# Feed-forward of a hybrid trunk layer on one core: eight block products or seven, all tokens at once or two sets of them

## The chip, the core and the metric

The kernel runs on one core of a Trainium2 chip. The engines are named as the profile names them: PE (matrix products, with PEld for its weight loads), DVE (vector engine), ACT (scalar engine), POOL (GpSimd) and SP (here only a queue of DMAs). The metric is the device time of one execution in microseconds, the median of several runs.

## The reference

One layer of a streaming trunk for 1040 prompt tokens (16 learned meta tokens and 1024 new ones) and 32 sample tokens, model width 1024, feed-forward width 2816. A token mixer (attention, pooling, a scan) comes first and is the same in both kernels. What the change touches is the second half of the layer:

```python
x = x + rmsnorm(mix @ w_out, ln_post_mix)
h = rmsnorm(x, ln_pre_ffn)
ff = (jax.nn.silu(h @ w_gate) * (h @ w_up)) @ w_down
x = x + rmsnorm(ff, ln_post_ffn)
```

All inputs are fp32. The feed-forward's result is needed for 1056 tokens (32 sample, 1024 prompt): the rows of the meta tokens are dropped.

## The kernel before

**Arithmetic.** Every fp32 operand of a product is split in two fp32r numbers, `hi` (a rounded copy, made on ACT by `hi_of`, line 47) and `lo` (the rest, made on DVE by `lo_of`, line 53, or on POOL by `lo_of_sbuf`, line 56). A product of two operands is three matmuls, hi·hi, hi·lo and lo·hi (`PASSES`, line 37), summed in PSUM.

**Stages.** Phase A is the in-projection, the scan and the pooling, phase B the attention, phase C the out-projection with both norms (lines 1215 to 1487), phase D the feed-forward (from line 1304). Phase C works on nine token tiles: 48 rows, then eight of 128. For each it takes the out-projection's products (`c_products`), adds, norms and scales on DVE, ACT and POOL, and turns the result with PE transposes (`c_turn`, line 1292) into `T`, features by tokens, split into hi and lo. `T` is first the out-projection's operand and then, tile by tile, the feed-forward's.

**Feed-forward.** The 2816 features are 22 tiles of 128, the tokens three chunks of 288, 384 and 384 (`FCH`). For a feature tile `f`, `gu_weights` (line 1385) loads gate and up weights, 512 KB each, and splits them: two copies of 128x1024 on ACT, two subtractions of 128x1024 on DVE. `gu_products` (line 1394) takes 24 matmuls for each chunk and each of gate and up; `gu_act` (line 1405) does silu on ACT, the product with up on DVE, and splits the result into `act`. For two feature tiles `down_weights` (line 1498) splits the down weights and `down` (line 1507) takes, for each chunk and each of the 8 tiles of outputs, six matmuls, whose result DVE adds to `acc` in SBUF (line 1520). The last two feature tiles go chunk by chunk, so that the ends of the token tiles (`final_tile`, `last_tile`) run beside products.

**Order.** Each engine executes its instructions in the order of its own list. PE's list in phases B and C is set by hand by the order of the code; the loops over the feed-forward are laid down in the order of the code, and a scheduler orders the other engines' lists. PSUM has eight banks: four for products of gate and up and for turns, four for the down products.

## Time and profile before

| | |
|---|---|
| median of 3 runs | 1409.21 us (1408.17 to 1415.13) |
| profiled execution | span 1416.8 us from its first to its last instruction; the page shows no other time for it |
| PE busy | 1322.6 us, 93% of the span |
| DVE, ACT, POOL busy | 639.2, 398.5, 205.1 us |
| feed-forward's matmuls in the profile | gate and up 3168, down 1536 and 36 at the end |
| first of them | at 626.59 us after the span's start |

Lines of a group of instructions read: source line, engine, operation, out<-in by the program's names, shape of the output and of the input, count, then busy time in us, mean ns of one, and the idle time of the engine just ahead of them with what ended it. Lines of the timeline read: start in us, duration in us (of the whole piece where several instructions are merged), engine, line, operation, and in brackets the idle time ahead of it. A table of windows gives for each stretch the busy us of every engine.

### The profile page before, as it was taken

Reading aid. Unit: us, or ns where it says so; the run is one execution under the profiler, and the core shown is the slowest. Engines: PE = TensorE matmul, PEld = TensorE weight load, DVE = VectorE, ACT = ScalarE, POOL = GpSimd, SP = SyncE. Lnnn points to the kernel's source line nnn. Section 1 sums busy time; section 2 is a strip of 40 time slices with the busy share of each in tenths; the row PEclk is TensorE's granted clock in tenths of the full one; section 3 lists DMA queues with packets and bytes.
Section 4 is the critical chain, followed back from the end, with each engine's and each line's share of the span. In section 5 each row is a group of like instructions: output and inputs, shape, how many; then the busy total and the mean of one; then the engine's idle time right before and its main releaser. Section 6 shows DMA issues by size and latency. Waiting matters only on the chain. (4 is left out here: it accounts for less than half of the span.)

```text
span 1416.8 us, 19972 instructions
## 1 busy us (share of the span) xinstructions
PE 1322.6 (93%) x7898; PEld 1236.0 (87%) x7898; DVE 639.2 (45%) x1209; ACT 398.5 (28%) x868; POOL 205.1 (14%) x311
## 2 busy tenths in 40 slices
PE   7999999999695596999999999999999999999996
PEld 6999788878574473779999999999999999999996
DVE  4578774554552141675525251515152424243356
ACT  7332442443543252443111111111111120212013
POOL 1001672101031221672000000000000000000024
PEclk9999999999897797999999999999999999999999
DMA  8320457989989835645111110111110111110024
GB/s 296 118 83 24 134 165 243 175 137 140 161 136 164 157 69 157 219 171 165 46 44 57 34 60 31 60 31 60 31 60 31 60 30 60 31 59 19 16 79 149
DMA packets 87089, 140.30 MB, mean 99 GB/s; under 512 B 19670, under 2 KB 63724, under 8 KB 86996
## 3 DMA queue, kind: packets, MB, share of 16 engines
q1 hardware_dynamic: 86996, 139.03, 38.7%
q8 instruction: 62, 1.02, 0.3%
q14 instruction: 31, 0.25, 0.1%
HBM read 103.66 MB, written 35.34 MB: 98 GB/s over the span
## 5 line engine op out<-in xcount | busy, mean ns | idle before, releaser
L60 PE MATMUL gu<-T,wgu 128*128 128x384 f32 (+1 forms) x3168 | 514.3, 323 | 1.9 <-ACT fs L1411 1.3
L60 PEld LDWEIGHTS gu<-T,wgu 128*128 128x128 f32 x3168 | 509.7, 188 | 2.5 <-ACT fs L1411 1.6
L60 PE MATMUL dn<-act,HD 128*128 128x384 f32 (+1 forms) x1536 | 248.1, 322 | 0.0
L60 PEld LDWEIGHTS dn<-act,HD 128*128 128x128 f32 x1536 | 246.4, 188 | 0.0
L60 PE MATMUL wk<-T,wkh 128*128 128x384 f32 (+1 forms) x1152 | 208.5, 334 | 1.3 <-POOL wkh L57 0.8
L60 PEld LDWEIGHTS wk<-T,wkh 128*128 128x128 f32 x1152 | 190.2, 192 | 4.4 <-POOL wkh L57 1.1
L1412 DVE TENSOR_TENSOR fs<-fs,gu 128x384 f32<-128x384 f32 (+1 forms) x66 | 34.3, 520 | 332.8 <-PE gu L60 332.6
L1520 DVE TENSOR_TENSOR acc<-acc,dn 128x384 f32<-128x384 f32 (+1 forms) x232 | 117.9, 518 | 86.3 <-PE dn L60 85.1
L69 POOL TENSOR_SCALAR est<-est 128x1 f32<-128x1 f32 (+1 forms) x9 | 3.6, 397 | 726.6 <-ACT ey L1324 723.0
L60 PE MATMUL o<-PT,H 128*128 128x256 f32 (+1 forms) x324 | 64.6, 316 | 26.7 <-ACT ot L1097 15.9
L54 DVE TENSOR_TENSOR PT<-t,PT 128x512 fp32r<-128x512 f32 (+2 forms) x96 | 50.4, 530 | 64.6 <-ACT PT L49 63.3
L49 ACT ACTIVATE HD<-dr 128x1024 fp32r<-128x1024 f32 x22 | 22.3, 1054 | 203.3 <-PE dn L60 200.2
L60 PEld LDWEIGHTS o<-PT,H 128*128 128x128 f32 x324 | 50.2, 208 | 33.6 <-ACT ot L1097 17.1
L49 ACT ACTIVATE act<-fs 128x384 fp32r<-128x384 f32 (+1 forms) x66 | 32.5, 493 | 160.3 <-DVE fs L1412 160.2
L1411 ACT ACTIVATE fs<-gu 128x384 f32<-128x384 f32 (+1 forms) x66 | 30.7, 465 | 162.8 <-PE gu L60 162.8
L49 ACT ACTIVATE wgu<-gr 128x1024 fp32r<-128x1024 f32 (+1 forms) x48 | 47.1, 982 | 72.7 <-PE gu L60 72.7
L60 PE MATMUL s<-H 64*128 64x512 f32 (+5 forms) x180 | 65.8, 378 | 0.9 <-DMA H<-qd 0.9
L49 ACT ACTIVATE PT<-t 128x512 fp32r<-128x512 f32 (+2 forms) x96 | 44.1, 468 | 79.7 <-PE t L1063 49.8
L60 PE MATMUL wp<-wo,T 128*128 128x512 f32 (+1 forms) x162 | 51.4, 443 | 14.3 <-ACT pp L931 14.3
L1018 DVE CUSTOM_DVE_ANT_0 S<-s,H,pinf 128x512 f32<-128x512 f32 (+4 forms) x54 | 34.6, 640 | 64.6 <-PE s L60 59.3
L1063 PE MATMUL t<-ident,S 128*128 128x128 f32 x264 | 48.0, 292 | 14.3 <-DVE st L1018 8.8
L1063 PEld LDWEIGHTS t<-ident,S 128*128 128x128 f32 x264 | 30.1, 143 | 26.7 <-issue 16.2
(231 smaller groups left out, 1347.2 us busy)
## 6 DMA issues: line engine op xcount, KB each, us to landing
gr<-in_wgu_dram SPq DMA_DIRECT2D x40, 512.0 KB, 4.7
dr<-in_wd_dram SPq DMA_DIRECT2D x22, 512.0 KB, 3.6
wkr<-in_wx_dram SPq DMA_DIRECT2D x16, 512.0 KB, 6.3
H<-qd SPq DMA_DIRECT2D x18, 268.0 KB, 7.2
xt<-in_x_dram SPq DMA_DIRECT2D x8, 512.0 KB, 7.0
wor<-in_w_out_dram SPq DMA_DIRECT2D x8, 512.0 KB, 7.3
ppd<-pp SPq DMA_DIRECT2D x8, 512.0 KB, 10.5
cp<-ppd SPq DMA_DIRECT2D x8, 512.0 KB, 3.9
```

What stands on the lines that cost most here:

```text
L49: nc.scalar.activation(out, in_, AF.Copy)
L54: nc.vector.tensor_tensor(out=out, in0=in_, in1=hi.bitcast(F32), op=ALU.subtract)
L60: return nc.tensor.matmul(out, lhsT, rhs, start=start, stop=stop, skip_group_check=True)
L69: gp.tensor_scalar(v, ssq, ssq2, n * EPS, op0=ALU.add, op1=ALU.add)
L1018: nc.vector.tensor_tensor_reduce(out=Sf[:R, PAD + j0:PAD + j0 + n], in0=ps[:R, :n], in1=bc[:R, k0 + j0:k0 + j0 + n].bitcast(F32), scale=1. ...
L1063: nc.tensor.transpose(ps[:, c:c + P], tiles[h, t][0][:, P * b:P * b + P], ident)
L1411: nc.scalar.activation(s[:, :n], pg[:, :n], AF.Silu)
L1412: nc.vector.tensor_mul(s[:, :n], s[:, :n], pu[:, :n])
L1520: nc.vector.tensor_add(dst, dst, ps[:, :n])
```

## The change

The feed-forward's three products are taken by a scheme of seven block products (the Strassen-Winograd form). Each matrix is cut in 2x2 blocks; sums and differences of blocks of each operand are formed, seven products are taken instead of eight, and sums of the products give the four result blocks.

- **Tokens** come in two sets, one after the other: set 0 has 544 tokens as two blocks of 272 (the sample tokens and prompt tiles 1 to 4), set 1 has 512 as two of 256 (tiles 5 to 8). Both sets go through all weights, so that all weights are loaded, summed and split twice.
- **Units.** A gate-up unit takes two feature tiles: 7 block products of 24 matmuls each (two halves f by four k by three passes), each [128x128] by [128x272] or [128x256]. A down unit takes four feature tiles (two in the first group of set 0 and in the last of set 1): 7 block products of 24 matmuls (12 in the two short ones). A set has 11 gate-up units and 6 down units, in the order gate-up, gate-up, down after the start.
- **Weights** (`w_steps`): per unit four loads of 512 KB, four sums of blocks on POOL (128x1024 each), seven splits, each a copy of 128x1024 on ACT and a subtraction of 128x1024 on DVE. They are made in seven steps, the first five beside the unit before.
- **Tokens' operand** (`h_steps`): four sums of blocks (DVE and POOL), seven splits of 128x1088 or 128x1024, once for each set. It lies in `T`, over the out-projection's operand. Set 1's blocks wait in DRAM (`h1d`).
- **Evictions.** In a gate-up unit, products 1 and 2 add up in one PSUM tile, 6, 7 and 4 in a second, 5 and 3 in a third; DVE or ACT reads each stage of the running sum before the next product goes on top of it. The results' four blocks give four more differences on POOL (128x272 or 128x256) and seven split blocks `AO`. In a down unit DVE adds 14 pieces of 128x544 or 128x512 from PSUM to `acc`, 7 blocks by 4 tiles.
- **Ends.** After the last down unit of a set seven sums of blocks of `acc` are made on DVE, and the token tiles end as before (`final_piece`): set 0's beside the first units of set 1, set 1's at the end of the program.
- Four small tiles of one column to nine become slices of one. Up to the middle of the out-projection every engine's list is otherwise the same in both kernels.

The core of the diff, with comment lines left out:

```diff
+FSET = (272, 256)
+ORDER7 = (1, 2, 6, 7, 4, 5, 3)
...
+    def h_steps(s, blocks, spare):
+        H = h_ops(s)
+        b11, b12, b21, b22 = blocks
+        dv, gp, sb = nc.vector, nc.gpsimd, ALU.subtract
+        def split(i, raw):
+            split_raw(H[:, i - 1, 0], H[:, i - 1, 1], raw)
+        split(1, b11)
+        dv.tensor_tensor(out=b11, in0=b12, in1=b11, op=sb)
+        yield
+        split(2, b21)
+        dv.tensor_tensor(out=spare, in0=b22, in1=b11, op=sb)
+        gp.tensor_tensor(out=b21, in0=b21, in1=spare, op=sb)
+        yield
+        split(6, spare)
+        gp.tensor_tensor(out=b12, in0=b22, in1=b12, op=sb)
...
+    def w_steps(unit, nm, W):
...
+        split_raw(*ring(1), a11)
+        gp.tensor_tensor(out=a11, in0=a11, in1=a21, op=ALU.subtract)
+        yield
+        split_raw(*ring(2), a12)
+        yield
+        s2 = S6[:, :na]
+        gp.tensor_tensor(out=s2, in0=a22, in1=a11, op=ALU.subtract)
+        gp.tensor_tensor(out=a12, in0=a12, in1=s2, op=ALU.subtract)
+        split_raw(*ring(6), s2)
+        gp.tensor_tensor(out=a21, in0=a21, in1=a22, op=ALU.add)
+        yield
+        split_raw(*ring(7), a11)
+        yield
+        for i in ORDER7[4:6]:
+            split_raw(*ring(i), a21 if i == 5 else a22)
+            yield
+        split_raw(*ring(3), a12)
+        yield
...
-    def gu_products(f, ci, g):
-        c0, n = FCH[ci]
-        ps = psum("mm", f"gu{f}_{g}_{c0}")
-        for k in range(NK):
-            for j, (i0, i1) in enumerate(PASSES):
-                mm(ps[:, :n], gus[f][:, i0, 8 * g + k], T[:, i1, k, c0:c0 + n],
-                   k == 0 and j == 0, k == NK - 1 and j == 2)
-        return ps
+    def gu_unit(s, W, p, par, between):
...
+        def prod(ps, i, start, after):
+            for f in range(2):
+                for k in range(4):
+                    for j, (i0, i1) in enumerate(PASSES):
+                        mm(ps[:, f, :n], W[i][:, i0, f, k * P:(k + 1) * P], H[:, i - 1, i1, k * n:(k + 1) * n],
+                           start and k == 0 and j == 0, k == 3 and j == 2)
+                after(ps[:, f, :n], f)
+            between()
+        def plus(out, other):
+            return lambda ps, f: dv.tensor_tensor(out=out[:, f], in0=ps, in1=other[:, f], op=add)
+        X = pair_psum("gx")
+        prod(X, 1, True, lambda ps, f: nc.scalar.activation(m1[:, f], ps, AF.Copy))
+        prod(X, 2, False, lambda ps, f: nc.scalar.activation(g0[:, f], ps, AF.Silu))
+        Y = pair_psum("gy")
+        prod(Y, 6, True, plus(u2, m1))
+        prod(Y, 7, False, plus(u3, m1))
+        prod(Y, 4, False, plus(m1, m1))
...
+        dv.tensor_tensor(out=m1, in0=g0, in1=m1, op=ALU.mult)
+        split(2, 4, m1)
+        Z = pair_psum("gz")
+        prod(Z, 5, True, plus(u3, u3))
+        def c12(ps, f):
+            plus(u2, u2)(ps, f)
+            nc.scalar.activation(u2[:, f], u2[:, f], AF.Silu)
+            dv.tensor_tensor(out=u2[:, f], in0=u2[:, f], in1=u3[:, f], op=ALU.mult)
+        prod(Z, 3, False, c12)
...
+        gp.tensor_tensor(out=t1, in0=b12, in1=b11, op=sb)
+        gp.tensor_tensor(out=t2, in0=b22, in1=t1, op=sb)
+        gp.tensor_tensor(out=t3, in0=b22, in1=b12, op=sb)
+        gp.tensor_tensor(out=t4, in0=b21, in1=t2, op=sb)
+        split(6, 8, g0)
+        split(4, 6, u3)
+        split(1, 2, u2[:, 1:2])
+    def down_unit(s, W, np_, first, between, after=None):
+        n = FSET[s]
+        for i in ORDER7:
+            for jj in range(2):
+                ps = pair_psum("dn")
...
+                dst = acc[:, i - 1, 2 * jj:2 * jj + 2, :n]
+                if first:
+                    nc.scalar.activation(dst, ps[:, :, :n], AF.Copy)
+                else:
+                    nc.vector.tensor_tensor(out=dst, in0=ps[:, :, :n], in1=dst, op=ALU.add)
...
+    def combine(s):
+        for o, x in ((2, 1), (6, 1), (3, 6), (7, 6), (4, 7), (3, 5), (5, 7)):
+            acc_add(s, o, x)
+            yield
...
+        def between():
+            n_between[0] += 1
+            step(preps[si])
+            if hgen is not None:
+                step(hgen)
+            if si == 0 and n_between[0] <= 3:
+                c_stage(8 + n_between[0], 5 + n_between[0])
+            if nxt is not None and n_between[0] > 2:
+                step(nxt)
+            if fin:
+                f = fin.pop(0)
+                f()
```

The lists of three engines show what moves. **DVE, in the middle of the feed-forward.** Before, for feature tiles 6 and 7: `HD<-dr` and `wgu<-gr` are subtractions for weights, `act` those for activations, `fs` the products of gate and up:

```order
L54 TENSOR_TENSOR HD_6119<-dr7_7945,HD_6119 128x1024
L54 TENSOR_TENSOR HD_6119<-dr8_8316,HD_6119 128x1024
L1412 TENSOR_TENSOR fs6_16_7651<-fs6_16_7651,gu6_1_16_7625 128x288
L54 TENSOR_TENSOR act6_7650<-fs6_16_7651,act6_7650 128x288
L1412 TENSOR_TENSOR fs6_304_7706<-fs6_304_7706,gu6_1_304_7681 128x384
L54 TENSOR_TENSOR act6_7650<-fs6_304_7706,act6_7650 128x384
L1412 TENSOR_TENSOR fs6_688_7761<-fs6_688_7761,gu6_1_688_7736 128x384
L54 TENSOR_TENSOR wgu8_8141<-gr8_0_8142,wgu8_8141 128x1024
```

Now, the second half of a gate-up unit (feature tiles 10 and 11) and the start of the next: `w0_gu12`, `HD` with `r0_gu12` are weights of the next unit, `AO0` split activations, `gy` and `gz` the PSUM tiles:

```order
L64 TENSOR_TENSOR w0_gu12_6_7876<-S6_5849,w0_gu12_6_7876 128x1024
L64 TENSOR_TENSOR AO0_5848<-HT_5225,T_66 128x544
L1538 TENSOR_TENSOR HT_5225<-gz_7883,HT_5225 128x272 x2
L64 TENSOR_TENSOR w0_gu12_7_7910<-r0_gu12_0_7809,w0_gu12_7_7910 128x1024
L1538 TENSOR_TENSOR HT_5225<-gz_7883,HT_5225 128x272
L1561 TENSOR_TENSOR HT_5225<-HT_5225 128x272
L1538 TENSOR_TENSOR HT_5225<-gz_7883,HT_5225 128x272
L64 TENSOR_TENSOR HD_5853<-r0_gu12_3_7813,HD_5853 128x1024
L1561 TENSOR_TENSOR HT_5225<-HT_5225 128x272
L64 TENSOR_TENSOR AO0_5848<-HT_5225,T_66 128x272
L64 TENSOR_TENSOR AO0_5848<-HT_5225,T_66 128x544 x2
L64 TENSOR_TENSOR HD_5853<-r0_gu12_2_7811,HD_5853 128x1024
```

The evictions of `gz`, on which the next products wait, now stand behind subtractions for the next unit's weights, and of these the one from `S6` waits for a sum on POOL. **POOL, in the feed-forward.** Before, its list goes from the norm of the last token tile in phase C straight to the ends of the token tiles in the last features:

```order
L67 TENSOR_SCALAR cst8_5740<-cst8_5740 128x1
L70 TENSOR_TENSOR cst8_5740<-cst8_5740,mhalf_69 128x1
L72 TENSOR_SCALAR cst8_5740<-cst8_5740 128x1
L76 TENSOR_SCALAR cst8_5740<-cst8_5740 128x1
L77 TENSOR_TENSOR cst8_5740<-cst8_5740 128x1
L69 TENSOR_SCALAR est0_11674<-est0_11674 32x1
```

Now, beside the same gate-up unit: four sums for the next unit's weights, the unit's four differences of activations (`HT`), four sums for the down unit after it:

```order
L1409 TENSOR_TENSOR r0_gu12_0_7809<-r0_gu12_0_7809,r0_gu12_2_7811 128x1024
L1414 TENSOR_TENSOR S6_5849<-r0_gu12_3_7813,r0_gu12_0_7809 128x1024
L1417 TENSOR_TENSOR r0_gu12_2_7811<-r0_gu12_2_7811,r0_gu12_3_7813 128x1024
L1415 TENSOR_TENSOR r0_gu12_1_7815<-r0_gu12_1_7815,S6_5849 128x1024
L1568 TENSOR_TENSOR HT_5225<-HT_5225 128x272
L1570 TENSOR_TENSOR HT_5225<-HT_5225 128x272
L1569 TENSOR_TENSOR HT_5225<-HT_5225 128x272
L1571 TENSOR_TENSOR HT_5225<-HT_5225 128x272
L1409 TENSOR_TENSOR r0_wd10_0_8039<-r0_wd10_0_8039,r0_wd10_2_8041 128x1024
```

POOL had nothing in this stage and now has eight sums for each gate-up unit and four for each down unit. **PE, from the out-projection into the feed-forward.** Before (`wo8` is the last tile's out-projection, `yT6` a turn, `gu` gate and up):

```order
L60 MATMUL wo8_1_5866<-wo4_5200,T_66 128x512 x3
L60 MATMUL gu0_0_16_5887<-T_66,wgu0_5340 128x288 x24
L1299 MATMUL yT6_0_5912<-ident_67,cx6_5561 128x128 x4
L1299 MATMUL yT6_1_5917<-ident_67,cx6_5561 128x128 x4
L60 MATMUL gu0_1_16_5945<-T_66,wgu0_5340 128x288 x24
```

Now:

```order
L70 MATMUL wo8_1_5823<-wo4_5197,T_66 128x512 x3
L70 MATMUL gx_5893<-T_66,w0_gu0_1_5870 128x272 x24
L1304 MATMUL yT6_0_5926<-ident_67,cx6_5561 128x128 x4
L1304 MATMUL yT6_1_5931<-ident_67,cx6_5561 128x128 x4
L70 MATMUL gx_5893<-T_66,w0_gu0_2_5877 128x272 x24
```

The order of the work is alike; but the `T` that `gx` reads is now written by `h_steps` over the operand that `wo8` still reads.

More of the change, by code (lines that the diff above doesn't have):

```diff
@@ L1403, in tile_hybrid_trunk @@
[L1403 to L1414 removed]
+            evac.append((t, b, ps))
@@ L1416, in c_steps, with pair_psum @@
+    def pair_psum(nm):
+        return psp[0].tile([P, 2, 512], F32, tag="pp", bufs=4, name=nm)
     def c_steps(n=1):
@@ L1571, in tile_hybrid_trunk @@
-    E2.release()
-    E.release()
+    for t in range(9):
+        ks = (3, 4) if t < 2 else (0, 1, 2, 3, 4)
+        c_wait(t, ks)
+        if 1 <= t < 8:
+            c_loads(t + 1)
+        c_products(t, 0, ks)
+        if t == 1:
+            rawq += [late_attn(2, *OCH[3])]
+        c_stage(t, t - 3 if t > 2 else None)
+        c_products(t, 1, ks)
+    while rawq or rawlive:
+        clock[0] += 400.0
+        steps()
+    order.__exit__(None, None, None)
+    WA.release()
+    WH.release()
@@ new lines, in tile_hybrid_trunk, with step @@
+    acc = None
+    def step(gen):
+        next(gen, None)
+    psp[0].release()
+    psp[0] = tc.alloc_tile_pool(name="psD", bufs=1, space=PSUM, reuse_waits="tile")
+    seq = [(s, u) for s in range(2) for u in units_of(s)]
+    Ws = [{} for _ in seq]
+    preps = [w_steps(u[1][0], f"{u[0]}_{u[1][0][0]}{u[1][0][1]}", Ws[i]) for i, u in enumerate(seq)]
+    first_h = h_steps(0, [HT[:, q] for q in range(4)], E.tile([P, 4 * FSET[0]], F32, name="hspare"))
+    for i in range(5):
+        step(preps[0])
+        if i < 2:
+            step(first_h)
```

416 lines of the change are left out of this document (202 added, 214 removed), and 3 rows, old and new, of the table PIECES.

## Prediction

> **What bounds the kernel now.** I read the page first, then the busy time by windows, the groups of instructions by shape, and the timeline where two engines meet. The page gives the share of each engine:
>
> ```profile
> span 1416.8 us, 19972 instructions
> PE 1322.6 (93%) x7898; PEld 1236.0 (87%) x7898; DVE 639.2 (45%) x1209; ACT 398.5 (28%) x868; POOL 205.1 (14%) x311
> ```
>
> The table of windows gives the feed-forward alone (busy us of each engine, then clock and DMA):
>
> ```profile
> core 0: us, PE busy (x) PEld busy (x) DVE busy (x) ACT busy (x) POOL busy (x), PEclk, DMA share, GB/s
> 800.00:1000.00 200.00, 200.00 (x1242) 200.00 (x1241) 71.75 (x122) 31.45 (x49) 0.00 (x0) 1.00 0.15 47
> ```
>
> PE is busy all 200 of 200 us, DVE 36%, ACT 16%, POOL never. So the feed-forward lasts as long as its matmuls, and fewer matmul columns are worth something as long as the other engines keep up. It begins at the row below, 626.59; up to there the lists of both kernels agree nearly, and I take that part as unchanged. The stage is 1416.8 − 626.6 = 790.2 us.
>
> ```profile
> 626.59 3.35 PE L60 MATMUL gu<-T,wgu 128*128 128x288 f32 x24
> ```
>
> **The matmuls: what is removed.** The groups by shape give a matmul's price at two widths:
>
> ```profile
> L60 PE MATMUL gu<-T,wgu 128*128 128x384 f32 x2112 | 374.9, 337 | 1.3 <-ACT fs L1411 1.3
> L60 PE MATMUL gu<-T,wgu 128*128 128x288 f32 x1056 | 143.9, 296 | 0.6 <-ACT wo L1262 0.6
> L60 PE MATMUL dn<-act,HD 128*128 128x384 f32 x1008 | 177.5, 336 | 0.0
> L60 PE MATMUL dn<-act,HD 128*128 128x288 f32 x528 | 72.2, 296 | 0.0
> L60 PE MATMUL dt<-HD,act 128*128 128x512 f32 x36 | 8.9, 399 | 0.0
> ```
>
> 374.9/2112 = 177.5 ns at 384 columns, 143.9/1056 = 136.3 at 288: 0.429 ns a column and 12.7 fixed. Carried on to the new widths that is 129.4 ns at 272 and 122.6 at 256. There will be 11 x 168 + 5.5 x 168 = 2772 of each, 358.7 + 339.8 = 698.5 us, in place of 374.9 + 143.9 + 177.5 + 72.2 + 8.9 = 777.4. PE saves 79 us; a unit of 168 matmuls lasts 21.7 us in set 0 and 20.6 in set 1.
>
> The Trainium skill (TensorE: Matmul & The Clock Gate, Back-to-back issue gap) gives N/2.4 + 2.5 ns for a matmul. By it the saving would be 708.8 − 623.7 = 85 us, an estimate from that page; the rows show the larger fixed part, and they decide.
>
> **What is added on DVE, ACT and POOL.** The prices, by the same view:
>
> ```profile
> L54 DVE TENSOR_TENSOR wgu<-gr,wgu 128x1024 fp32r<-128x1024 f32 x40 | 48.8, 1220 | 4.7 <-ACT wgu L49 4.7
> L54 DVE TENSOR_TENSOR act<-fs,act 128x384 fp32r<-128x384 f32 x44 | 24.4, 555 | 14.2 <-ACT act L49 14.2
> L54 DVE TENSOR_TENSOR act<-fs,act 128x288 fp32r<-128x288 f32 x22 | 10.1, 458 | 10.7 <-ACT act L49 10.7
> L1520 DVE TENSOR_TENSOR acc<-acc,dn 128x384 f32<-128x384 f32 x152 | 84.2, 554 | 77.5 <-PE dn L60 77.5
> L1520 DVE TENSOR_TENSOR acc<-acc,dn 128x288 f32<-128x288 f32 x80 | 33.8, 450 | 8.8 <-PE dn L60 7.5
> L49 ACT ACTIVATE wgu<-gr 128x1024 fp32r<-128x1024 f32 x40 | 42.2, 1054 | 72.7 <-PE gu L60 72.7
> L57 POOL TENSOR_TENSOR HX<-wor,HX 128x512 fp32r<-128x512 f32 x6 | 7.6, 1289 | 9.4 <-ACT HX L49 9.4
> L57 POOL TENSOR_TENSOR T<-or,T 128x256 fp32r<-128x256 f32 x9 | 6.5, 729 | 16.6 <-ACT T L49 16.6
> ```
>
> DVE takes 1.01 ns a column and 0.167 us fixed: 0.44 us at 272, 0.72 at 544, 0.685 at 512, 1.27 at 1088; the adds from PSUM go at the same rate. POOL takes 2.19 ns a column: 0.76 us at 272, 2.41 at 1024 (no row has it that wide).
>
> A gate-up unit of set 0: on DVE from SBUF alone seven weight splits, 7 x 1.22 = 8.54, three products 0.72 + 2 x 0.44, four splits of activations 3 x 0.72 + 0.44, together 12.7 us; with one operand in PSUM ten adds, 4.4. On POOL 4 x 2.41 + 4 x 0.76 = 12.7. ACT has 7 x 1.054 and about 13 narrow ones, 12 to 13 us. Each engine alone stays under PE's 21.7. In set 1 both sums are 12.6. A down unit has 8.5 from SBUF and 14 x 0.72 = 10.0 from PSUM on DVE, 9.6 on POOL.
>
> The weights are loaded twice; a load of 512 KB lands in 4.7 us and the DMA share now is 0.15, so twice that hides beside a unit.
>
> ```profile
> gr<-in_wgu_dram SPq DMA_DIRECT2D x40, 512.0 KB, 4.7
> ```
>
> **What these engines do to each other** decides. The timeline of the out-projection, where POOL and DVE meet:
>
> ```profile
> 613.43 1.28 DVE L1273 SCALAR_TENSOR_TENSOR cx<-cx,cst,gpm 128x1024 f32<-128x1024 f32 x1 [0.80 <-POOL cst L77]
> 615.63 1.95 POOL L57 TENSOR_TENSOR wgu<-gr,wgu 128x512 fp32r<-128x512 f32 x1
> 616.35 1.27 DVE L54 TENSOR_TENSOR T<-yT,T 128x512 fp32r<-128x512 f32 x2
> 621.82 1.29 POOL L57 TENSOR_TENSOR wgu<-gr,wgu 128x512 fp32r<-128x512 f32 x1
> 621.90 2.29 DVE L1273 SCALAR_TENSOR_TENSOR cx<-cx,cst,gpm 128x1024 f32<-128x1024 f32 x1 [0.80 <-POOL cst L77]
> 646.17 1.69 POOL L72 TENSOR_SCALAR cst<-cst 128x1 f32<-128x1 f32 x1
> 646.21 1.23 DVE L54 TENSOR_TENSOR HD<-dr,HD 128x1024 fp32r<-128x1024 f32 x1 [0.49 <-ACT HD L49]
> 647.36 0.45 DVE L54 TENSOR_TENSOR act<-fs,act 128x288 fp32r<-128x288 f32 x1
> ```
>
> The scaling takes 1.28 us alone, and 2.29 where a POOL subtraction began just ahead of it: it ends 1.08 after POOL's end at 623.11. So a DVE instruction with both operands in SBUF waits for the whole POOL instruction, and only 0.20 of its start is hidden. With one operand in PSUM it doesn't wait: two turns' splits take 0.635 each at 616.35 beside POOL. The reverse: at 646.17 a POOL instruction of one column takes 1.69 us, until two chained DVE subtractions are over.
>
> The Trainium skill (SBUF — State Buffer, SBUF: two separate sides) states this as an exclusive lock on a pair of ports, held for the whole instruction by whichever starts first. The rows agree, but for two chained DVE instructions, which kept it; by the rule alone nothing of the next one's start is hidden and a unit's sum is the 25.4 below, by the rows some is hidden, down to 23.0.
>
> So a gate-up unit needs these ports for 12.7 + 12.7 = 25.4 us (set 1: 25.1), more than PE's 21.7. If each of POOL's eight instructions hides 0.15 at both ends it is 23.0 (22.7); if PSUM adds never run beside POOL, 12.7 + 4.4 + 12.7 = 29.8 (29.3). I take 25.4: the hidden starts about pay for the adds that come in between. Nothing evens it out between units, as DVE's list puts the evictions PE waits for behind splits that need the unit's own sums from POOL: a PSUM tile isn't free for the next product until its add is done. A down unit needs the ports 8.5 + 9.6 = 18.2 us and goes at PE's pace.
>
> Sum of the units: 11 x (25.4 + 25.1) + 5.5 x (21.7 + 20.6) = 788 us. Beside it:
>
> - **Start.** The split tokens go where the out-projection's operand was, so nothing can be split ahead of its end. DVE's list up to the first add from `gy` is 7 splits and 2 sums of 1.27, 5 weight splits of 1.22, and 2.7 for the last token tile: 20.2 us. PE would need that add after 9.8 (two products, two turns, half a product): 10.4 late, with POOL's four sums on the ports (2 x 2.41 + 2 x 2.55) 20.3. I take 15.3. Before, three chunks of products covered the last tile.
> - **Change of sets.** In the last down unit of set 0 come 7 splits and 2 sums of 1024 on DVE, 2 sums on POOL: 15.8 us on the ports, less the 3.5 that unit has free: 12.3.
> - **End of set 0**, beside set 1's first units: 7 sums of 1.27 and 6 pieces with an add on DVE (0.685) and on POOL (1.29): 20.7. Before, PE's products hid such ends; ports that are always wanted don't.
> - **Last unit**: DVE has 14 x 0.685 adds, 7 sums of 1.2 and some 2 us of splits, 20 us, for 10.3 us of products: 9.8.
> - **After the last product**: 10.8 us before (from 1398.75 + 7.22 to 1416.8), and a second tile stands behind it, two scalings, two adds: 14.
>
> ```profile
> 1389.73 1.03 PE L1312 MATMUL eT<-ident,acc 128*128 128x128 f32 x8
> 1398.75 7.22 PE L60 MATMUL dt<-HD,act 128*128 128x512 f32 x30
> L1329 DVE SCALAR_TENSOR_TENSOR ey<-eT,est,gpo 128x512 f32<-128x512 f32 x10 | 7.0, 745 | 7.4 <-POOL est L77 7.4
> ```
>
> 788 + 15 + 12 + 21 + 10 + 14 = 860 us in place of 790: 70 longer. The profiled execution's span is 1416.8, 7.6 over the median of the runs; I put the difference on the median: 1409 + 70 = 1479 us.
>
> **Rivals.**
>
> *PE sets the pace after all* (faster). If POOL's instructions fall into DVE's waits for PE, or hold the ports more briefly than at 512 columns, units go at PE's pace: 698.5, the 88 turns at 1.03 for eight 11.3, start 10.4, change of sets 5, last unit 9.8, end 14: 749, 41 less, 1368 us. For it: DVE idled 64% of the stage. Against: 12.7 + 12.7 is over 21.7 at every price I can read. It decides below 21.7 us a unit. By the page's gap for matmuls it would be 6 us less.
>
> *Both about even* (no change). Every start hidden, 23.0 and 22.7, half of the change of sets and of set 0's end covered by down units: 735 + 15 + 6 + 10 + 10 + 14 = 790, 1409 us.
>
> *All in a row* (slower still). DVE's evictions stand behind splits that wait for POOL, and PSUM adds never run beside it: 29.8 and 29.3 a unit, 650 + 233 + 72 = 955, 1574 us. It decides if the chain from sum to split to add is longer than the ports' sum.
>
> That fewer products are not what happens can be ruled out: the lists show the matmuls counted above.
>
> **How the numbers follow.** Port-bound units 0.53, all in a row 0.10, PE's pace 0.23, about even 0.14 (of which 0.09 lies within 0.5%, about what a measurement here can tell from no change, 0.02 below and 0.03 above). Faster 0.25, same 0.09, slower 0.66. The forecast's own range is 23.5 to 28 a unit, 1425 to 1540. Down to 1365 it takes in rather more than half of PE's pace; left out are the rest of it and most of the longest case, some 0.2.
>
> **What would show it.** Right: DVE's subtractions of 128x1024 well over 1.22 us on the mean, POOL's sums over 2.41, PE idle ahead of `gy` and `gz` matmuls with DVE as releaser, gate-up units 25 us apart and down units 21 to 22; PE at 272 and 256 columns near 129 and 123 ns where it runs. Wrong: PE at 95% or more in the feed-forward, DVE's means at 1.22 beside a busy POOL; or idle PE that waits for ACT, DMA or weights instead.

## The result, and the profile after

The changed kernel takes 1856.73 us (median of four runs, 1853.03 to 1865.75), the kernel before 1412.17 beside it (1408.17 to 1418.64): a ratio of 1.315, with a 95% interval of 1.310 to 1.320. The forecast was 1479, slower, and at most 1540. The sign was right, the size was not: the change costs 445 us, not 70.

The page of the profiled execution (its span is 1855.1 us), the line of shares:

```profile
PE 1422.0 (77%) x8710; PEld 1273.8 (69%) x8710; DVE 1066.2 (57%) x1526; ACT 633.4 (34%) x1160; POOL 645.0 (35%) x539
```

The windows, first the same 200 us of the feed-forward, then all of it (busy us of PE, PEld, DVE, ACT and POOL, then clock and DMA):

```profile
800.00:1000.00 200.00, 152.39 (x981) 141.19 (x981) 118.18 (x135) 60.15 (x79) 78.37 (x40) 0.88 0.19 61
627.00:1855.00 1228.00, 871.93 (x5648) 806.59 (x5648) 735.94 (x821) 384.78 (x554) 480.24 (x303) 0.85 0.21 68
```

PE was busy all of 200 us before and is busy 152 now; DVE, the busiest beside it, 118. No engine is full: something makes them wait for each other in turn. Over the stage PE idles 1228 − 872 = 356 us. It is busy 872 us for products that were priced at 698.5: in part since the granted clock is 0.85 on the mean, in part for the turns (some 11 us) and for the ends of half products that stand alone, which the unit below shows.

The groups by shape in the feed-forward (mean ns of one, then the idle time just before the group and what ended it):

```profile
L64 DVE TENSOR_TENSOR HD<-r_gu,HD 128x1024 fp32r<-128x1024 f32 x78 | 126.9, 1631 | 72.0 <-ACT HD L59 71.7
L1417 POOL TENSOR_TENSOR r_gu<-r_gu,r_gu 128x1024 f32<-128x1024 f32 x21 | 67.7, 3222 | 0.0
L1538 DVE TENSOR_TENSOR HT<-gy,HT 128x272 f32<-128x272 f32 x60 | 26.3, 438 | 58.3 <-PE gy L70 57.8
L1553 DVE TENSOR_TENSOR HT<-HT 128x544 f32<-128x544 f32 x10 | 22.8, 2278 | 0.3
```

The ports are fought over as forecast: DVE's subtractions of 1024 columns take 1.63 us (1.22 alone), POOL's sums up to 3.22, and the product of 544 columns at L1553 takes 2.28 where 0.72 was its price. The adds from PSUM are at 0.438, just as priced. But 1.63 for 1.22 is some 3 us in a unit of seven, and the units are 13 us longer than forecast. The timeline of PE through one gate-up unit of set 0 shows the rest (start, duration, matmuls in a row, and in brackets the wait ahead of them and who ended it):

```profile
926.68 1.75 PE L70 MATMUL gx<-T,w_gu 128*128 128x272 f32 x12
928.92 1.77 PE L70 MATMUL gx<-T,w_gu 128*128 128x272 f32 x12 [0.49 <-ACT HT L1541]
...
933.44 1.77 PE L70 MATMUL gx<-T,HD 128*128 128x272 f32 x12 [0.49 <-ACT HT L1542]
935.05 1.67 PE L70 MATMUL gy<-T,HD 128*128 128x272 f32 x12
937.90 1.77 PE L70 MATMUL gy<-T,HD 128*128 128x272 f32 x12 [1.19 <-DVE HT L1538]
...
944.82 1.77 PE L70 MATMUL gy<-T,w_gu 128*128 128x272 f32 x12 [0.53 <-DVE HT L1538]
948.30 1.77 PE L70 MATMUL gy<-T,w_gu 128*128 128x272 f32 x12 [1.71 <-DVE HT L1538]
949.91 1.66 PE L70 MATMUL gz<-T,w_gu 128*128 128x272 f32 x12
955.23 3.09 PE L70 MATMUL gz<-T,w_gu 128*128 128x272 f32 x12 [3.66 <-DVE HT L1538]
958.95 3.06 PE L70 MATMUL gz<-T,HD 128*128 128x272 f32 x12 [0.63 <-DVE HT L1538]
962.54 3.09 PE L70 MATMUL gz<-T,HD 128*128 128x272 f32 x12 [0.53 <-DVE HT L1538]
965.43 2.61 PE L70 MATMUL gx<-T,HD 128*128 128x272 f32 x12
```

The unit takes 965.43 − 926.68 = 38.75 us. Three things are to be read here. First, PE stops after every half product of 12 matmuls, about 0.5 us, until the engine that evicts has read what was just written; only where a new PSUM tile begins (`gy` at 935.05, `gz` at 949.91, the next unit's `gx` at 965.43) does it go on. Even the second half of a product waits, though it goes to another bank than the first. Second, three waits are longer: 1.19, 1.71, 3.66. Third, after the longest one a half product takes 3.1 us instead of 1.77. The unit's eleven waits sum to 10.8 us; with 21.7 of products at full clock, 6.3 are left: 3.9 for the three slow half products, the rest for the ends of the others (1.77 us each, where 12 matmuls at the forecast's price are 1.55).

DVE and POOL around the longest wait:

```profile
950.10 2.38 POOL L1415 TENSOR_TENSOR r_gu<-r_gu,S 128x1024 f32<-128x1024 f32 x1
950.12 0.44 DVE L1538 TENSOR_TENSOR HT<-gy,HT 128x272 f32<-128x272 f32 x1 [1.87 <-PE gy L70]
950.59 2.47 DVE L1553 TENSOR_TENSOR HT<-HT 128x544 f32<-128x544 f32 x1
952.98 1.21 DVE L64 TENSOR_TENSOR w_gu<-S,w_gu 128x1024 fp32r<-128x1024 f32 x1
954.12 0.71 DVE L64 TENSOR_TENSOR AO<-HT,T 128x544 fp32r<-128x544 f32 x1
954.75 0.43 DVE L1538 TENSOR_TENSOR HT<-gz,HT 128x272 f32<-128x272 f32 x1
```

The add that PE waits for (954.75) could have begun at 951.6, when the first half of `gz` was done. It stands behind a product that POOL's sum holds until 952.5, a split for the next unit's weights, and a split of activations. So three theories stand against each other: A, the halves in series; B, the ports; C, the clock that falls; and beside them D, the order of DVE's and ACT's lists.

### The profile page after: what moved, and what is told of

Same layout as the page of the kernel before. It is cut to its first block, busy times and chain, and to the rows that moved or that the text cites. A ratio compares the mean times of both kernels' runs of the same rounds, so it can differ in the third digit from the quotient of the medians.

```text
span 1855.1 us, 22934 instructions
## 1 busy us (share of the span) xinstructions
PE 1422.0 (77%) x8710; PEld 1273.8 (69%) x8710; DVE 1066.2 (57%) x1526; ACT 633.4 (34%) x1160; POOL 645.0 (35%) x539
## 5 line engine op out<-in xcount | busy, mean ns | idle before, releaser
L70 PE MATMUL gy<-T,HD 128*128 128x272 f32 (+1 forms) x984 | 148.5, 303 | 70.0 <-DVE HT L1538 67.8
L70 PEld LDWEIGHTS gy<-T,HD 128*128 128x128 f32 x984 | 132.1, 199 | 84.3 <-DVE HT L1538 80.9
L64 DVE TENSOR_TENSOR HD<-r_gu,HD 128x1024 fp32r<-128x1024 f32 x78 | 126.9, 1631 | 72.0 <-ACT HD L59 71.7
L70 PE MATMUL gz<-T,HD 128*128 128x256 f32 (+1 forms) x600 | 122.4, 374 | 52.4 <-DVE HT L1538 52.4
L70 PEld LDWEIGHTS gz<-T,HD 128*128 128x128 f32 x600 | 111.1, 270 | 62.1 <-DVE HT L1538 51.4
L70 PE MATMUL dn<-AO,HD 128*128 128x272 f32 (+1 forms) x708 | 142.3, 295 | 4.5 <-DVE AO L64 2.3
L70 PE MATMUL gx<-T,HD 128*128 128x256 f32 (+1 forms) x600 | 98.8, 321 | 51.2 <-ACT HT L1541 38.6
L70 PEld LDWEIGHTS gx<-T,HD 128*128 128x128 f32 x600 | 88.7, 218 | 60.9 <-ACT HT L1541 43.9
L1538 DVE TENSOR_TENSOR HT<-gy,HT 128x256 f32<-128x256 f32 (+1 forms) x126 | 54.1, 429 | 119.1 <-PE gy L70 118.5
L70 PEld LDWEIGHTS dn<-AO,HD 128*128 128x128 f32 x708 | 117.6, 198 | 6.8 <-DVE AO L64 4.1
L70 PEld LDWEIGHTS gx<-T,w_gu 128*128 128x128 f32 x456 | 70.2, 225 | 71.7 <-ACT HT L1541 22.8
L70 PE MATMUL dn<-T,HD 128*128 128x272 f32 (+1 forms) x408 | 109.4, 299 | 7.6 <-ACT T L59 4.5
```

The lines of the kernel that those rows point to most:

```text
L64: nc.vector.tensor_tensor(out=out, in0=in_, in1=hi.bitcast(F32), op=ALU.subtract)
L70: return nc.tensor.matmul(out, lhsT, rhs, start=start, stop=stop, skip_group_check=True)
L1538: return lambda ps, f: dv.tensor_tensor(out=out[:, f], in0=ps, in1=other[:, f], op=add)
```

## The experiments

Each was timed beside the kernel before on the same chip; "over before" is the difference there (the change itself: 444.6 us). Behind the change, which has four runs, the first seven have one each, the last five medians of four to six.

| kernel | us | over before |
|---|---|---|
| the change | 1856.7 | 444.6 |
| halves apart | 1665.6 | 262.2 |
| no sums of weights | 1724.1 | 320.7 |
| halves apart, no sums | 1482.6 | 79.2 |
| halves apart, sums on DVE | 1575.1 | 171.7 |
| gaps filled | 1835.1 | 437.0 |
| spread order, sums on DVE | 1540.1 | 142.0 |
| spread order, sums on POOL | 1597.5 | 199.4 |
| second spread order, sums on DVE | 1520.6 | 120.1 |
| the same, no sums | 1444.2 | 43.7 |
| the same, sums on DVE, without the end of set 0 | 1485.5 | 85.0 |
| the same, sums on DVE, without set 1's splits | 1501.9 | 101.4 |
| second spread order, sums on POOL | 1573.0 | 172.5 |

**Halves apart.**

```diff
-        X = pair_psum("gx")
+        X = [pair_psum(f"gx{f}") for f in range(2)]
...
-                        mm(ps[:, f, :n], W[i][:, i0, f, k * P:(k + 1) * P], ...
+                        mm(ps[f][:, 0, :n], W[i][:, i0, f, k * P:(k + 1) * P], ...
```

> Edit: each half (256 of 512 features) of a gate-up product gets a PSUM tile of its own; nothing else is changed, and the whole computation stays. In the changed kernel a gate-up unit of set 0 takes 38.75 us (926.68 to 965.43), and its matmuls stop after almost every half product of 12: three waits of 0.49 for ACT, eleven halves with DVE as releaser, most of 0.53, and 1.2, 1.7 and 3.7 where DVE is late. Theory A (halves in series): PE waits for the eviction of the half just finished, because both halves lie in one tile; with tiles of their own the other half (1.6 us) covers it. Then about 0.5 x 10 goes, 1.6 comes off each longer wait, and some of the cold matmuls go: 27 to 30 us a unit, 22 units, about 1856 - 22 x 10 = 1640 us (1560 to 1690). Theory B (the prediction's ports): what PE waits for is DVE behind POOL's sums; shorter waits elsewhere are only filled by longer ones, 36 us a unit or more, 1790 to 1860 us. Theory C (the cold clock is what costs, whatever the gaps): the waits fall but the slow matmuls of the second half of a unit stay, 33 us, about 1730.

It takes 182 us off, inside theory A's range. PE in a gate-up unit (872.86 to 902.80, 29.9 us):

```profile
878.94 6.17 PE L70 MATMUL gy<-T,HD 128*128 128x272 f32 x48
...
887.96 3.17 PE L70 MATMUL gz<-T,w_gu 128*128 128x272 f32 x24
897.22 5.75 PE L70 MATMUL gz<-T,HD 128*128 128x272 f32 x24 [6.09 <-DVE HT L1538]
```

The half-microsecond waits are gone: 48 matmuls run in one go, 3.0 us for 24. So the half of a pair waited for the other half's eviction only because both lay in one tile, whose accesses are tracked as one; the data asks only that the next product wait for it. The longest wait grew, from 3.66 to 6.09: DVE is now later against a PE that comes earlier. Theory A holds for its part, B and C as the sole cause fall. The 182 us hold what the clock gives back with the gaps (0.895 granted over the run in place of 0.878), which isn't taken apart, and the four pair tiles now hold two products at a time instead of four.

The Trainium skill (Perfetto Trace Analysis, Matmuls) asks that independent groups of matmuls go round the PSUM banks, so that an eviction lies beside the next group. Here the halves already lay in two banks, and that alone covered nothing; in two tiles it was worth 182 us.

**No sums of weights**, with the halves as in the change, and then both edits together.

```diff
-        gp.tensor_tensor(out=a11, in0=a11, in1=a21, op=ALU.subtract)
...
-        gp.tensor_tensor(out=s2, in0=a22, in1=a11, op=ALU.subtract)
-        gp.tensor_tensor(out=a12, in0=a12, in1=s2, op=ALU.subtract)
-        split_raw(*ring(6), s2)
-        gp.tensor_tensor(out=a21, in0=a21, in1=a22, op=ALU.add)
+        split_raw(*ring(6), a22)
```

> Edit: POOL's four sums of weights a unit are left out (five of the seven block products then use plain blocks; this part of the computation is wrong by it), splits and all products stay. Takes away POOL's 10.8 to 11 us a unit on the ports and the chain from sum to split. Theory A (halves in series): the waits of 0.49 to 0.54 stay, only the late ones shrink (1.7 to 0.53, 3.7 to about 2, and the cold matmuls behind it partly): 3 to 6 us a unit, 1720 to 1790 us. Theory B (ports set the pace): units fall to PE's pace of 21.7 us plus a little, 33 units near 22 to 25 us and the ends as they are, 1450 to 1550 us. Theory C (cold clock): between them, since the wait that makes PE cold goes, about 1650.

> Both edits together: halves in tiles of their own, and POOL's sums of weights left out (five of seven block products use plain blocks). If A and B each hold a part, this is near PE's pace in the units: 33 units of 21.7 or 20.6 us and the ends (start, change of sets, last unit), 700 + 60 to 90, 1390 to 1450 us. If something else holds PE (the ring of five weight tiles, ACT's order), it stays over 1500 us.

Without the sums 124 us go, with the half-microsecond waits all still there, as A said:

```profile
902.19 1.77 PE L70 MATMUL gy<-T,w_gu 128*128 128x272 f32 x12 [0.53 <-DVE HT L1533]
903.79 1.66 PE L70 MATMUL gz<-T,w_gu 128*128 128x272 f32 x12
907.37 1.77 PE L70 MATMUL gz<-T,w_gu 128*128 128x272 f32 x12 [1.92 <-DVE HT L1533]
```

Both together take 365 off, more than 182 + 124: each cost had hidden part of the other. The 1390 to 1450 that I expected for both was missed by 33 us; order accounts for about as much, since the same work in the second spread order, below, is 43.7 us over before and not 79.2.

**Halves apart, sums on DVE.**

```diff
-        gp = nc.gpsimd
+        gp = nc.vector
```

> Halves in tiles of their own, and the four sums of weights of a unit on DVE instead of POOL; the whole computation stays. DVE then has 11 splits and sums of 1.22 us, 4.4 us of adds from PSUM, 4 to 5 us of activations, 22 to 23 us a gate-up unit with nothing to lock against but POOL's four of 0.77. Theory B: a unit falls from 25.4 (the ports' sum) to DVE's 22 to 23, so this is 50 us faster than the halves alone. Theory A alone: DVE is fuller and its evictions later, the time is within 40 us of the halves alone, on either side. Estimate 1500 to 1620 us.

90 us faster than the halves alone, though DVE now has four more instructions of 1.22 us a unit: a sum that runs on POOL costs DVE and PE more than doing it on DVE. Two waits are left in each unit, and neither is mainly for a port. Their rows, from two units in a row:

```profile
867.43 5.51 PE L70 MATMUL gz<-T,HD 128*128 128x272 f32 x24 [3.81 <-DVE HT L1538]
...
880.95 1.77 PE L70 MATMUL gx<-T,HD 128*128 128x272 f32 x12 [3.49 <-ACT HT L1541]
```

At `gz` two sums, a split and a product stand on DVE between the last eviction of `gy` and this one; at `gx` ACT's copy stands behind splits of activations that wait for POOL's four differences, one of which takes 1.74 us beside a DVE split in place of 0.77.

**Gaps filled**, on the change as it was, to price the clock by itself:

```diff
+                for _ in range(FILL.get((i, f), 0)):
+                    mm(fillps[0], W[i][:, 0, f, :P], H[:, i - 1, 0, :256], True, True)
```

> Edit on the changed kernel: ahead of the half products that wait, PE does matmuls of 256 columns into a PSUM tile of its own, which nobody reads (4 where the wait was 0.5 us, 9, 13 and 28 where it was 1.2, 1.7 and 3.7 us; 82 a gate-up unit, about 10 us, as much as PE idles there); the pair tiles are 3 instead of 4 for it. The waits, the ports and DVE's list stay, only PE's gaps are filled. Theory C (the clock pays for the gaps): in the feed-forward PE is busy 872 us for products that need 698.5 and transposes of 11 at the full clock, so 162 us are cold matmuls; with the gaps filled the granted clock goes back to 0.97 or more and 80 to 150 us of it come back, 1700 to 1780 us. Rival: DVE, ACT and POOL set when a half product may start, so that warmer matmuls only wait longer, and fillers that are longer than their gap add: 1830 to 1900 us.

The window of 200 us, beside 152.39 and 0.88 in the change, and a wait that grew (2.26 us at this place in the change):

```profile
800.00:1000.00 200.00, 183.28 (x1333) 172.94 (x1332) 119.63 (x137) 60.85 (x81) 80.20 (x40) 0.97 0.18 62
961.21 3.06 PE L70 MATMUL gx<-T,HD 128*128 128x272 f32 x12 [2.77 <-ACT HT L1547]
```

The clock is back at 0.97 here, and the time over before is 8 us less, about what one run can tell (from the first `gx` to the end of the span it is 1204.8 us in place of 1223.9). In the units of set 0 behind the first group, a gate-up unit gets 2.3 us shorter on the mean (35.1 to 40.8 in place of 37.1 to 42.9), some 50 us if all 22 do. The rest of the slow matmuls' time comes back as waits: `gx` waits 2.77 us for ACT although four fillers stand ahead of it. Part of what was won is lost again: a down unit, with three pair tiles instead of four, takes 25.0 to 25.8 us in place of 23.4 to 23.8, and the start is 7 us longer. So by this edit, which also takes a pair tile away, C is worth some 50 us in the gate-up units, and its 80 to 150 don't come. Its 162 us of cold matmuls were too many to begin with, since the ends of half products are in them.

The Trainium skill (TensorE: Matmul & The Clock Gate, Terms) puts the loss from a throttled clock at the throttled time by the share of pulses left out. By that rule the mean clock of 0.85 would cost 1228 x 0.15 = 184 us, an estimate from that page of the skill. PE's busy time is some 160 us over its price, not all of it for the clock; with the clock at 0.97 the kernel got 8 us back.

**Spread order.** One sum or split behind each half product's eviction, by a table; the last splits of a unit's activations behind the next unit's first products; in steady units DVE and ACT keep the order of the code:

```diff
+    OWN = {(0, 0): ["B"], (0, 1): ["s7"], (1, 0): ["D"], (1, 1): ["s4"], (2, 0): ["s5"], (2, 1): ["s3"]}
+    NEXT = {(1, 0): ["L11"], (2, 0): ["L22"], (2, 1): ["L21"], (3, 0): ["L12"], (3, 1): ["s1"], (4, 0): ["A"],
+            (5, 0): ["s2"], (5, 1): ["S"], (6, 0): ["s6"]}
...
                 after(ps[f][:, 0, :n], f)
+                tick(f)
```

(`s` are splits, `A`, `S`, `D`, `B` the four sums, `L` loads; the key is product and half.)

> Halves in tiles of their own, the sums of weights on DVE, and the preparation of weights spread by hand: one split or sum of 1024 columns behind each half product's eviction instead of up to five in a row ahead of the evictions from gz, the last splits of a unit's activations put behind the next unit's first products, DVE's and ACT's lists kept in the order written (but in the first unit, around the change of sets and in the last unit). The whole computation stays. Theory D (what is left in the units is order: evictions behind lumps of splits, 3.8 us at gz, 3.5 at gx): DVE has 22 us of work in a gate-up unit and 23.5 in a down unit, and with no lumps a unit takes 22 to 24 us; with the ends as they are (about 95 us, from the run without sums) 735 + 95, a total of 1440 to 1490 us. Rival (DVE is simply full, or the wait for ACT's halves holds it): units stay at 25 to 31 us, 1550 to 1600 us.

> The same spread order, with the four sums of weights of a unit on POOL as in the changed kernel. This is the case that the prediction reckoned: no halves in series, no lumps, only the ports between DVE and POOL. Ports' sum: 12.7 + 12.7 = 25.4 us a gate-up unit (23 to 29.8), down units 22 to 23; 11 x (25.4 + 25.1) + 5.5 x (22.5 + 21.5) + 95 = 893 us behind 626, about 1520 (1470 to 1600), 50 to 90 us over the same with sums on DVE. If the lock costs more than the sum of the two (a locked DVE instruction delays the next eviction, and that PE), 1600 to 1660, as with the halves alone. If the lock costs nothing once the order is good, within 20 us of the sums on DVE.

With sums on DVE 30 us less than in the old order; the time lies in neither of the two ranges expected. The first gate-up unit of a group goes at PE's pace (844.13 to 866.39), the second takes 28 us, with this wait in it:

```profile
870.43 3.27 PE L70 MATMUL gx<-T,HD 128*128 128x272 f32 x24 [0.87 <-ACT HT L1538]
873.54 3.17 PE L70 MATMUL gy<-T,w_gu 128*128 128x272 f32 x24
880.00 5.78 PE L70 MATMUL gy<-T,w_gu 128*128 128x272 f32 x24 [3.29 <-DVE HT L1535]
```

DVE there waits 2.10 us for a split of the last unit's activations, which waits for POOL's sums of them in a row; a sum and more splits follow before the eviction. With the weights' sums on POOL 57 us more, inside the 50 to 90 of the ports' theory, its total at the upper end of their range.

**Second spread order**, then the same without sums, without the end of set 0, without set 1's splits:

```diff
+    TAIL = {"gu": {(2, 0): 0, (2, 1): 1, (3, 0): 2}, "wd": {(0, 0): 2, (1, 1): 0, (2, 0): 1}}
+    ORD = {"gu": ORDER7, "wd": (1, 2, 3, 6, 7, 4, 5)}
```

The three others each change one thing more in it:

```diff
-            "A": lambda: tt(out=R[0], in0=R[0], in1=R[2], op=ALU.subtract),
+            "A": lambda: None, "S": lambda: None, "D": lambda: None, "B": lambda: None,
...
-                comb = combine(s)
-                fin += [lambda c=comb: [step(c) for _ in range(4)], lambda c=comb: [step(c) for _ in range(4)]]
...
-            hgen = h_steps(1, blocks, tmps[par % 2][:, :4 * FSET[1]])
+            hgen = None
```

> The spread order with sums on DVE, with two more edits: after a gate-up unit that is followed by another, the last splits of its activations come one and a half products later, behind POOL's four sums; and in a down unit the third product is the one whose activations need no sum on POOL. The whole computation stays. In the spread order the first gate-up unit of a group takes 22 us, the second 27 to 28 (PE waits 3.3 us for an eviction from gy that stands on DVE behind the split that waits for POOL) and the down unit 24.4 (2.25 us for the same split). If that chain is what is left, the second unit falls to 23 and the down unit to 23.5: 10 x 4.5 + 10 x 1 = 55 us, about 1485 us (1460 to 1510). If DVE's 22 to 24 us of work a unit are the limit and the wait was only where it showed, 1520 to 1545.

> The same order without the four sums of weights of a unit (five of seven block products use plain blocks). DVE has 17 us a unit, nothing on POOL but four narrow sums: the units should go at PE's pace, 22.0 and 21.0 us with what the evictions leave, 33 units of 11 x 22 + 11 x 21 + 5.5 x 22.5 + 5.5 x 21.5 = 715 us. What is then over 626 + 715 are the ends alone: start, change of sets, end of set 0, last unit, tail. The prediction has 72 us for them (with 698.5 of products 1409 or no gain at all), the run of halves without sums suggested 93: 1415 by the first, 1436 by the second. In both cases the kernel is not faster than before even with its products at full pace. Rival: faster than 1395, the ends are smaller when DVE has room.

> The second spread order without the end of set 0: the seven sums of accumulators and the five pieces of normalisation, residual and store of the first set are left out (their outputs aren't written). It prices one term of the prediction, which had 20.7 us for it. In the spread order the first two units of set 1 with these pieces between them take 80 us in place of 2 x 21 to 25: by that the term is 30 to 38 us. Expected 20 to 38 us less than the second spread order; under 15 if the wait there is for set 1's own splits and not for the end.

> The second spread order without the splits of set 1's tokens (four loads, seven splits and four sums left out; the products of set 1 use set 0's operand). It prices the change of sets, 12.3 us in the prediction. The last down unit of set 0 takes 32 us in the spread order in place of 24.4, so 8 us there, and what the next unit waits besides. Expected 8 to 15 us less than the second spread order; 0 to 4 if it is hidden beside the end of set 0.

The windows of one group of two gate-up units and a down unit in set 0, first with sums on DVE, then without sums:

```profile
837.00:911.00 74.00, 66.61 (x508) 65.00 (x507) 65.05 (x83) 29.53 (x41) 10.99 (x8) 0.98 0.27 86
```

```profile
813.00:878.00 65.00, 64.15 (x505) 63.22 (x504) 50.44 (x70) 29.55 (x41) 10.01 (x8) 1.00 0.30 98
```

With sums on DVE the two gate-up units even out at about 25 us each, and the gain is 22 us, not 55: DVE is busy 65 of 74 us, and the total lies at the lower edge of the rival's range (DVE's own work is the limit). That DVE is the limit isn't shown by this: it idles 9 of the 74 us, PE 7. Without sums PE is busy 64 of 65 us, 129 ns a matmul: that is PE's pace, and it shows the ends alone. The rows where the regular units begin and stop in that kernel:

```profile
613.02 0.59 PE L70 MATMUL gx<-T,w_gu 128*128 128x272 f32 x1 [10.75 <-ACT T L59]
...
681.93 3.26 PE L70 MATMUL gx<-T,HD 128*128 128x272 f32 x24 [3.36 <-ACT acc L1598]
...
990.65 0.29 PE L70 MATMUL dn<-T,HD 128*128 128x272 f32 x1
...
1096.41 0.28 PE L70 MATMUL dn<-T,HD 128*128 128x256 f32 x1
...
1390.85 0.28 PE L70 MATMUL dn<-T,w_wd 128*128 128x256 f32 x1
```

Its span is 1440.0 us. What ends the wait of 10.75 us ahead of the first product, with the last product of the out-projection above it:

```profile
600.71 1.55 PE L70 MATMUL wo<-wo,T 128*128 128x512 f32 x6
609.24 0.60 ACT L1271 ACTIVATE wo<-cx 128x512 f32<-128x512 f32 x1 [5.42 <-DVE cx L1270]
611.86 2.10 ACT L59 ACTIVATE T<-HT 128x1088 fp32r<-128x1088 f32 x2
```

The first product waits for ACT's first copy of the tokens' operand. That copy stands in ACT's list behind the last token tiles' norms (L1271), for which ACT itself waits 5.42 us. Every one of the changed kernels has this wait, 10.7 us; the kernel before has none there (626.59). From the out-projection's end at 602.27 the start lasts 79.7 us for 32.6 of products and 2.4 of turns: 45 over. From the last down unit of set 0 to the third unit of set 1 it is 105.8 us for 62.9 of products and 4.8 of turns: 38 over. The end is 49.1 us for 10.3 of products: 39 over. Together 122 us (products by the prices of the prediction, a turn at 0.8 us). The kernel is 44 us slower than before (ratio 1.032, 1.027 to 1.037) with its products at PE's pace: over both sums I had written, and no rival's 1395.

Left out, the end of set 0 gives back 35 us and set 1's splits 19; both were forecast smaller, 21 and 12, and the second is over the 8 to 15 that I expected here. They overlap: in the second spread order with sums on DVE, which has both, the stretch around the change of sets is 44 us over its products and turns.

**Second spread order, sums on POOL.** The edit is `nc.gpsimd` for `nc.vector` in the sums of weights.

> The second spread order with the four sums of weights of a unit on POOL, the whole computation: the case of the prediction with both other costs (halves in series, evictions behind lumps) out of the way. With sums on DVE a group of two gate-up units and a down unit takes 72 us in set 0 and 71 in set 1, without sums 65.6 and 63.6. The prediction's ports: gate-up units 25.4 and 25.1, down units at PE's pace of 21.7 and 20.6 (23 as measured), so groups of 73 to 74 and 71 to 73, about as long as with sums on DVE: 1520 to 1545 us. If instead every POOL sum pushes back the evictions that stand behind the locked DVE instruction, as in the first spread order (57 us more than with sums on DVE, groups of 78 to 79 us), 1565 to 1600.

1573 us, in the second range. PE where two gate-up units and a down unit of set 0 begin, and the next group:

```profile
852.00 3.24 PE L70 MATMUL gx<-T,w_gu 128*128 128x272 f32 x24 [1.53 <-DVE acc L1603]
...
877.96 6.18 PE L70 MATMUL gx<-T,HD 128*128 128x272 f32 x48
...
902.64 0.29 PE L70 MATMUL dn<-T,w_wd 128*128 128x272 f32 x1
...
927.43 1.74 PE L70 MATMUL gx<-T,HD 128*128 128x272 f32 x12 [1.53 <-DVE acc L1603]
```

Gate-up units of 25.96 and 24.68 us, a down unit of 24.79: 75.4 for the group. The first unit's longest wait, with DVE's rows ahead of it:

```profile
869.46 3.39 DVE L64 TENSOR_TENSOR HD<-r_gu,HD 128x1024 fp32r<-128x1024 f32 x1
872.77 0.78 DVE L1540 TENSOR_TENSOR HT<-gz,HT 128x272 f32<-128x272 f32 x2
873.35 4.78 PE L70 MATMUL gz<-T,HD 128*128 128x272 f32 x24 [2.69 <-DVE HT L1540]
```

One split that POOL's sum holds for 3.39 us in place of 1.22 stands ahead of the eviction. So here the ports cost by what a held instruction pushes back, as the second range had it, and not by the sum of their work.

## Why the prediction was wrong

In the profiled execution of the change, from the last product of the out-projection on (620.50), the stage is 1234.6 us where the forecast had 860: 374 over. Of these, 253 lie in the four groups of each set (two gate-up units and a down unit) that are away from the start, the change of sets and the end; 38 lie in the start, 67 around the change, 16 at the end. By cause they are the 182, 90 and 102 us below. The sign came out as forecast with the forecast's mechanism in it for a part only: moving POOL's sums to DVE gives back 52 to 90 us of the 445.

- **PE's price was right to 3%.** 129.4 ns at 272 columns was forecast. In a row matmuls go at 125.2 (48 from 878.94 to 884.95 with the halves apart); with the small gaps of a group it is 65.17 us for 504, 129.3 (813.00 to 878.17 without sums).
- **The prices on DVE and POOL were right, and so was it that they hold each other up.** L1538 takes 0.438 us (0.44), and L1553 takes 2.28 beside POOL's sums in place of 0.72. The gate-up unit of 25.4 us by the ports' sum comes out near the last experiment, 24.7 to 27.3 in the units of set 0 behind the first group and 25.1 to 28.1 in set 1. But that match is no proof, and in part luck: with the sums on DVE, where the same reckoning gives 12.7 + 4 x 1.22 + 4 x 0.76 = 20.6, the units take 24.1 to 25.5 in set 0.
- **The step that failed** is "a PSUM tile isn't free for the next product until its add is done", with no price of its own. The sentence was right, and its cost was taken as paid within the ports' sum. In the change PE waits for that add after each half product, since a pair of banks is one tile: 182 us, shown by the halves apart. It could be read from PE's own list, which has the wait at the second half. (The first two lines are the first half of `gz`, the next two the second.)

```
L70 MATMUL gz<-T,HD 128x272 [waits PE_49]
L70 MATMUL gz<-T,HD 128x272 x11
L70 MATMUL gz<-T,HD 128x272 [waits DVE_49]
L70 MATMUL gz<-T,HD 128x272 x11
```

- **The second failure is in the same paragraph**: evictions behind splits that wait for POOL were named, quoted from DVE's list, and then not priced, as if the lists ran as the sum of their work. Put in a spread order with the same work on the same engines, the kernel goes from 262 to 172.5 us over before: 90 us. The rival "all in a row" had this mechanism, at a chance of 0.10 and 29.8 us a unit; measured were 37 to 46 in set 0 behind the start, since it lacked the halves.
- **What is left** is 172.5 − 70 = 102 us. The profiled execution of the last experiment is 108 over the forecast's 860 from the out-projection's end (612.31) on, and these rows cut it:

```profile
695.98 4.80 PE L70 MATMUL gx<-T,HD 128*128 128x272 f32 x24 [3.91 <-ACT acc L1601]
...
1002.96 6.26 PE L70 MATMUL gx<-T,HD 128*128 128x272 f32 x48 [1.53 <-DVE acc L1603]
...
1207.81 5.79 PE L70 MATMUL gx<-T,w_gu 128*128 128x256 f32 x48
...
1509.60 3.08 PE L70 MATMUL gx<-T,HD 128*128 128x256 f32 x24 [1.92 <-DVE acc L1603]
```

Four groups up to 1002.96 and four from 1207.81 to 1509.60 take 608.8 us, where the forecast had 4 x 72.5 + 4 x 70.8 = 573: 36 over, some 20 of them in the down units (23.3 to 24.8 us and 22.8 to 23.1, not PE's pace). The splits and sums of the last gate-up unit's activations fall into these. The start is 32 over, the stretch around the change of sets 28, the end 11. The start was the term most under-sized: its 15 us had PE's first two products go at once, and left out that they wait for ACT's copies. In the kernel at PE's pace the ends are 122 us where the forecast's five terms have 72.
- **Against the list of what would show it.** Right: DVE's means over 1.22, POOL's over 2.41 for three of a gate-up unit's four sums (though for one of a down unit's), PE idle ahead of `gy` and `gz` by DVE. Off: down units of 23.4 us for 21 to 22. Wrong: gate-up units 25 us apart; they were 37 to 46 in set 0 behind the start. Also PE waits for ACT ahead of `gx`, which the list had under "wrong".
- **The faster rival** (PE's pace, 1368 us) can't be had by mending the units: at PE's pace the kernel is at 1444, since the ends give back more than the 79 us of products that the seven blocks save. A version that beats the kernel before wasn't found; the best with the whole computation is the second spread order with sums on DVE, at 1.085 (1.080 to 1.089).

What stays open: the 182 and 124 us don't add up to the 365 of both, and how the 59 between them divide was not taken apart. What holds the units at 24 to 25 us with the sums on DVE isn't shown either. Nor was a start tried in which set 0's splits begin earlier, since their operand lies where the out-projection's still is.

## What to carry to other kernels

When a running sum is read between its steps, ask what PE does in the microsecond after each step: give each bank a tile of its own, so that the read lies beside the other half's matmuls. A sum of work on each engine is a lower bound; the list of an engine that evicts must be priced as a list, with what stands ahead of each eviction and what that waits for. And count the ends of every pass: two passes over the tokens have a start, a change and an end. Here these cost 122 us at PE's pace, more than the 79 us of products that the scheme saves; the kernel before has 13 (a stage of 790 us for 777 of products).

## What the runs showed of the hardware

- The granted clock fell among short gaps. In the unit shown it is 1.00 from 926.68 to 953.80 and 0.50 from 955.23 to 965.43, where the half products take 3.1 us in place of 1.77, still so at 962.54, after gaps of 0.63 and 0.53 only. In a later unit it is 1.00 from 1029 to 1052 and 0.50 from 1053 to 1056, and the longest wait until then is 1.73 us. With filled gaps it was 0.97 in place of 0.88, for some 50 us in the gate-up units and 8 us of the kernel.
- From the last matmul of a half product to the first of the next, over an add of 0.44 us on DVE, PE idles 0.53 us; over a copy of 0.40 us on ACT it idles 0.49. That is what one step from PE to another engine and back cost here.
- A sum of 1024 columns cost this kernel less on DVE (1.22 us) than beside it on POOL (2.4 to 3.4 us): moving four a unit from POOL to DVE took 90 us off in the old order, 57 and 52 in the two spread ones.
